# Two-norm prologue of the second block: squares summed on VectorE alone, scaled X in a right-hand pool

## The chip, the cores and the metric

The kernel runs on one core of one Trainium2 chip. The metric is device microseconds of one execution; times of several executions are given by their median. A core has TensorE (PE in the rows, its weight loads PEld), VectorE (DVE), ScalarE (ACT), GpSimd (POOL) and SyncE (SP, which here only issues DMAs). Each engine works through its own queue in order and waits for others by semaphores.

## The reference, cut to what matters

Two model blocks run one after the other on x of 512 positions by 1024 features. The first ends with an expert layer (PEER) and a norm, the second begins with a gated feed-forward layer (FFN) behind a norm of its own:

```python
x = x + gate2 * peer(h2, ...)
x = rmsnorm(x, final_g)                      # end of the first block
x = x + 0.5 * swiglu(rmsnorm_2(x, ffn1_norm), w_gate, w_up, w_down)   # start of the second

def rmsnorm(x, g):
    return x * rsqrt(mean(x * x) + EPS) * g
def swiglu(x, w_gate, w_up, w_down):
    return (silu(x @ w_gate) * (x @ w_up)) @ w_down
```

After it come an attention mixer, a second FFN and a last norm. The two norms at the seam follow directly on each other: the first one's scale is common to a position, so both can be had from two sums over features, of x squared and of (final_g x) squared.

## The kernel before

X lies in SBUF as 8 tiles of 128 features by 512 positions (`X[0]` to `X[7]`). All large products are done in fp32 as three matmuls of rounded halves: `mm3` (lines 102 to 105) multiplies weights `whi`, `wlo` with activations hi, lo. Weights are streamed by SyncE in pieces of 128x1024 into `raw` (3 buffers); `split` (lines 98 to 100) makes `whi` of a piece on ScalarE (L99) and `wlo` on VectorE (L100), each with 3 buffers. `Lin.product` accumulates two PSUM banks `mm` over the 8 feature chunks, that is 48 matmuls from two pieces of weights; there are four `mm` banks.

At the seam, in the order of the program text: VectorE adds the expert layer's result to X (L913); `gains` (lines 203 to 209) makes `gh` on ScalarE (L206) and `gl` on VectorE (L207), the two halves of X times both norms' gains, 16 tiles of 128x512 in the pool `gpool`; `square_two` makes 16 squares on ScalarE (L953), eight with the gain (list `l`) and eight without (list `h`), and adds them up (L955), `l` on VectorE and `h` on GpSimd, 7 adds each. The squares borrow tiles of the FFN's hidden layer, whose pool `ffn` is on the right-hand side of SBUF. `rstd_two` sums each total over partitions by a matmul with ones (L158, first `h`, then `l`), and makes from them `rstd` (both norms together, L963 to L967) and `r3` (the first norm alone, L968 to L970). `scale_x` multiplies X by the first norm (L975, 8 instructions).

In `ffn`, the norm's scale is applied after the products: the gate product of the first 256 hidden columns runs on unscaled `gh`, `gl`; then `rstd` is called; then the up product runs; then `ev_g` (L1025) reads the gate banks from PSUM times `rstd`, and `ev_u` (L1030) the up banks. So with four banks TensorE can do two products before it needs `rstd`; the third waits until L1025 has read the first bank.

This part of the program isn't ordered by hand: a scheduler sets each engine's order from dependences and its own estimates of durations. Pools are stacked from the left or the right end of SBUF, and a tile that lies where an older one lay waits for the older one's last use.

Of the kernel before, what the change touches and what calls it, by code (L numbers as in the profile page):

```python
# [7 lines left out]
F32 = mybir.dt.float32  # L8
# [4 lines left out]
AF = mybir.ActivationFunctionType  # L13
# [5 lines left out]
S = 512  # L19
D = 1024  # L20
P = 128
# [37 lines left out]
def body(nc, tc, A, out, stop=None):  # L59
    from contextlib import ExitStack  # L60
    top = ExitStack()
    pool = lambda stack, name, bufs=1, **kw: stack.enter_context(
        tc.tile_pool(name=name, bufs=bufs, reuse_waits="tile", **kw))
# [11 lines left out]
    tmp = _Tmp()  # L75
# [12 lines left out]
    epst = eps2[:, 0:1]  # L88
# [3 lines left out]
    def col(name, c):  # L92
        o, w = VCOLS[name]
        return vec[:, o + c:o + c + 1]
# [60 lines left out]
    def fsum(ps, chunks):  # L155

        for n, c in enumerate(chunks):
            nc.tensor.matmul(ps, ones, c, start=n == 0, stop=n == len(chunks) - 1)  # L158
        return ps
# [159 lines left out]
    for k in range(DC):  # L319
        if k + 2 < DC:  # L320
            load(k + 2)
        h = tmp.tile([P, S], F32, tag="ht", name="ht", bufs=2)
# [183 lines left out]
    R = lambda stack, name, bufs=1, **kw: pool(stack, name, bufs, side="right", **kw)  # L506
# [11 lines left out]
    for c in range(DC):  # L518
        h = tmp.tile([P, S], F32, tag="ht", name="ht", bufs=2)
# [402 lines left out]
    st2 = ExitStack()  # L922
# [2 lines left out]
    pat = pool(st2, "pat", 1, space=PSUM)  # L925
    lin = Lin(st2, wbufs=3, psum=pmm)
    mp = pool(st2, "mix")
    gpool = pool(st2, "gains")

    def finish():  # L930
        st2.close()
# [8 lines left out]
    def sbank():  # L940

        return pat.tile([P, S], F32, tag="s", name="sum", bufs=2)

    r3 = mp.tile([P, S], F32, name="r3")

    squares = {}

    def square_two(fp):

        for name, eng in (("l", nc.vector), ("h", nc.gpsimd)):  # L950
            for c in range(DC):
                q = fp.tile([P, S], F32, tag=f"hd{name}{FC - 1 - c}", name="sq")
                nc.scalar.activation(q, X[c], AF.Square, scale=col("final_g", c) if name == "l" else 1.0)  # L953
                if c:
                    eng.tensor_add(squares[name], squares[name], q)  # L955
                else:
                    squares[name] = q

    def rstd_two():

        p3 = fsum(sbank(), [squares["h"]])
        sq = tmp.tile([P, S], F32, tag="sd", name="sd", bufs=1)
        nc.vector.tensor_scalar(sq, p3, EPS, EPS * EPS * D, op0=ALU.mult, op1=ALU.add)  # L963
        nc.vector.tensor_add(sq, sq, fsum(sbank(), [squares["l"]]))
        nc.scalar.activation(sq, sq, AF.Sqrt, scale=1.0 / D)
        r = tmp.tile([P, S], F32, tag="rstd", name="rstd", bufs=1)
        nc.vector.reciprocal(r, sq)  # L967
        sd3 = tmp.tile([P, S], F32, tag="ht", name="sd3", bufs=2)  # L968
        nc.scalar.activation(sd3, p3, AF.Sqrt, bias=epst, scale=1.0 / D)
        nc.vector.reciprocal(r3, sd3)  # L970
        return r

    def scale_x():
        for c in range(DC):
            nc.vector.scalar_tensor_tensor(X[c], X[c], col("final_g", c), r3, op0=ALU.mult, op1=ALU.mult)  # L975

# [37 lines left out]
    def ffn(i, hs, rstd, before=None, then=None):  # L1014

        fs = ExitStack()
        fp = R(fs, "ffn")
        hid = [None] * FC
        sl = {}
        if before:  # L1020
            before(fp)

        def ev_g(m, ps):
            sl[m] = fp.tile([P, S], F32, tag="sl", name="sl", bufs=3)
            nc.vector.tensor_mul(sl[m], ps, r)  # L1025
            nc.scalar.activation(sl[m], sl[m], AF.Silu)

        def ev_u(m, ps):
            t = tmp.tile([P, S], F32, tag="ht", name="ht", bufs=2)
            nc.vector.tensor_mul(t, ps, r)  # L1030
            nc.vector.tensor_mul(t, t, sl.pop(m))
            hid[m] = pair(fp, "hd", m)
            split(hid[m][0], hid[m][1], t)
        r = None
        for j in range(FF // 256):
            pg_ = lin.product(A[f"ffn{i}_w_gate_2"], DC, lambda k: hs[k], j)
            r = r or rstd()
            pu_ = lin.product(A[f"ffn{i}_w_up_2"], DC, lambda k: hs[k], j)
            for n in range(2):
                ev_g(2 * j + n, pg_[n])  # L1040
            for n in range(2):
                ev_u(2 * j + n, pu_[n])
            if j == 0 and then:
                then()
            if j == 4 and then:
                mixer_inputs()
        q = Sum2(DC, direct=0 if i == 1 else 2)

        def ev_d(m, ps):
            nc.vector.scalar_tensor_tensor(X[m], ps, 0.5, X[m], op0=ALU.mult, op1=ALU.add)  # L1050
            q.add(X[m])
        lin(A[f"ffn{i}_w_down_2"], FC, lambda k: hid[k], range(4), ev_d)
        fs.close()
        return q

    q = ffn(1, hs, rstd_two, square_two, scale_x)
    if stop == "f1":
        return finish()
# [125 lines left out]
    q = Sum2(DC, direct=0)  # L1184
# [16 lines left out]
    q = ffn(2, hs, lambda: qm.rstd(sbank(), D))  # L1201
# [83 lines left out]
```

## Time and profile before

| | |
|---|---|
| runs | 2621.91, 2624.31, 2623.8 us; median 2623.8 us |
| profiled execution | 2624.25 us, its span 2622.5 us |
| TensorE busy | 2551.2 us, 97% of the span |
| VectorE, ScalarE, GpSimd busy | 1797.8, 1054.8, 425.5 us |
| mean granted TensorE clock | 0.988 of full |
| last of the expert products to the third FFN product | 1579 to 1632 us |

Times in rows are microseconds from the start of the span. "Granted clock" is the share of TensorE's full 2.4 GHz that was granted. In a timeline row the bracket says how long the engine had been idle and whose event ended that; rows of one kind that follow each other are merged with their count.

### The profile page before, as it was taken

The numbers are of one execution on the slowest core, as the hardware profiler recorded it, in microseconds if no ns is written. First come the engines' busy times: TensorE is split into PE (matmuls) and PEld (weight loads), VectorE is DVE, ScalarE is ACT, GpSimd is POOL, SyncE is SP. The second block draws the span as 40 slices with busy tenths as digits, with TensorE's granted clock in tenths as the row PEclk, the third lists the DMA queues.
The fourth block names the chain that finished last, engine by engine and source line by source line (L and its number), as shares of the span: only waits on it lengthen the run. The fifth ranks groups of instructions, "written<-read, shape, count | busy, mean of one in ns | idle before, by whom it ended". The sixth has DMA issues, their size and how long they took to land.

```text
span 2622.5 us, 33272 instructions
## 1 busy us (share of the span) xinstructions
PE 2551.2 (97%) x12311; PEld 2148.2 (82%) x12311; DVE 1797.8 (69%) x3120; ACT 1054.8 (40%) x1759; POOL 425.5 (16%) x323
## 2 busy tenths in 40 slices
PE   8989799999999999999999998999999999999998
PEld 5867589999999988888888886878888675788886
DVE  7999878888987577778888788444334675544423
ACT  4324333467688533333333335222222554422221
POOL 0000231122221233343344321000010000100000
PEclk9999899999999999999999999999999999999999
DMA  7226621678888999999999972222333221222232
GB/s 269 92 94 203 228 73 65 230 237 286 286 293 306 348 362 338 335 330 331 350 340 356 333 284 75 97 89 96 89 97 108 89 73 45 89 96 97 89 96 73
DMA packets 212469, 509.09 MB, mean 194 GB/s; under 512 B 18577, under 2 KB 95889, under 8 KB 212306
## 3 DMA queue, kind: packets, MB, share of 16 engines
q1 hardware_dynamic: 161186, 353.39, 39.7%
q0 software_dynamic: 36864, 134.23, 14.2%
q10 hardware_dynamic: 14256, 19.33, 2.0%
q8 instruction: 97, 1.59, 0.2%
q14 instruction: 66, 0.54, 0.1%
HBM read 461.49 MB, written 45.39 MB: 193 GB/s over the span
## 4 chain that ended last, share of the span: by engine, by line
PE 86%; DVE 7%; ACT 3%; DMA 2%; issue 2%; ACTq 0%; DVEq 0%; SPq 0%
PE mm L103 14%; PE mm L105 14%; PE mm L104 14%; PE pv L105 7%; PE pv L104 7%; PE pv L103 7%; PE act L103 5%; PE act L104 5%; PE act L105 5%; PE mm L338 2%; PE pg L738 2%; PE s L1098 1%; DVE ycv L350 1%; ACT oa L727 1%; PE o L1123 1%
## 5 line engine op out<-in xcount | busy, mean ns | idle before, releaser
L99 ACT CAST whi<-raw 128x1024 fp32r<-128x1024 f32 x228 | 235.5, 1035 | 658.3 <-PE mm L104 537.0
L100 DVE TENSOR_TENSOR wlo<-raw,whi 128x1024 fp32r<-128x1024 f32 x212 | 256.8, 1213 | 326.1 <-ACT whi L99 320.7
L103 PE MATMUL act<-h2h,uhi 128*128 128x384 f32 x1024 | 347.1, 339 | 4.3 <-ACT ga L664 4.1
L104 PE MATMUL mm<-gl,whi 128*128 128x512 f32 x864 | 344.5, 399 | 2.5 <-DVE gl L207 2.4
L105 PE MATMUL mm<-gh,wlo 128*128 128x512 f32 x864 | 342.7, 397 | 1.5 <-DVE wlo L100 1.5
L103 PE MATMUL mm<-gh,whi 128*128 128x512 f32 x864 | 342.5, 397 | 0.4 <-DVE x L913 0.4
L105 PE MATMUL act<-h2h,ulo 128*128 128x384 f32 x1024 | 342.8, 335 | 0.0
L104 PE MATMUL act<-h2l,uhi 128*128 128x384 f32 x1024 | 342.5, 335 | 0.0
L105 PE MATMUL pv<-vhi,cl 128*128 128x512 f32 x768 | 299.6, 390 | 0.0
L104 PE MATMUL pv<-vlo,ch 128*128 128x512 f32 x768 | 299.5, 390 | 0.0
L103 PE MATMUL pv<-vhi,ch 128*128 128x512 f32 x768 | 298.7, 389 | 0.0
L848 DVE TENSOR_TENSOR vlo<-vraw,vhi 128x1024 fp32r<-128x1024 f32 x128 | 156.4, 1222 | 131.6 <-ACT vhi L842 128.8
L694 POOL DMA_INDIRECT row<-in_u_dram,idx x128 | 158.3, 1236 | 526.4 <-DVE act L677 456.8
L694 POOL DMA_INDIRECT row<-in_v_dram,idx x128 | 175.0, 1367 | 284.4 <-DVE gacc L685 262.3
L842 ACT CAST vhi<-vraw 128x1024 fp32r<-128x1024 f32 x128 | 134.4, 1050 | 185.4 <-issue 169.5
L100 DVE TENSOR_TENSOR ulo<-uraw,uhi 128x1024 fp32r<-128x1024 f32 x128 | 156.0, 1220 | 72.7 <-ACT uhi L99 67.7
L103 PEld LDWEIGHTS act<-h2h,uhi 128*128 128x128 f32 x1024 | 192.4, 188 | 7.6 <-ACT ga L664 6.3
L104 PEld LDWEIGHTS mm<-gl,whi 128*128 128x128 f32 x864 | 162.4, 188 | 44.1 <-DVE gl L207 3.8
L103 PEld LDWEIGHTS mm<-gh,whi 128*128 128x128 f32 x864 | 162.3, 188 | 42.6 <-issue 2.3
L105 PEld LDWEIGHTS mm<-gh,wlo 128*128 128x128 f32 x864 | 162.4, 188 | 41.2 <-issue 2.0
L178 POOL TENSOR_TENSOR sq<-sq 128x512 f32<-128x512 f32 x24 | 40.0, 1665 | 952.9 <-ACT sq L172 952.2
L104 PEld LDWEIGHTS act<-h2l,uhi 128*128 128x128 f32 x1024 | 192.4, 188 | 1.3
(835 smaller groups left out, 4884.1 us busy)
## 6 DMA issues: line engine op xcount, KB each, us to landing
uraw<-in_uT_dram SPq DMA_DIRECT2D x128, 512.0 KB
vraw<-in_v_dram SPq DMA_DIRECT2D x128, 512.0 KB
raw<-in_w_in_dram SPq DMA_DIRECT2D x52, 512.0 KB
gsc<-st SPq DMA_DIRECT2D x96, 256.0 KB
vg<-gsc SPq DMA_DIRECT2D x32, 768.0 KB
raw<-in_ffn_w_gate_dram SPq DMA_DIRECT2D x44, 512.0 KB
raw<-in_ffn_w_up_dram SPq DMA_DIRECT2D x44, 512.0 KB
raw<-in_ffn_w_down_dram SPq DMA_DIRECT2D x40, 512.0 KB
```

The source lines that it names most:

```text
L99: nc.scalar.copy(hi, src)
L100: (lo_eng or nc.vector).tensor_sub(lo, src, hi.bitcast(F32))
L103: nc.tensor.matmul(ps, whi, ahi, start=first, stop=False)
L104: nc.tensor.matmul(ps, whi, alo, start=False, stop=False)
L105: nc.tensor.matmul(ps, wlo, ahi, start=False, stop=last)
L178: self.eng.tensor_add(self.acc, self.acc, t)
L338: nc.tensor.matmul(first[m], w[:, m // 2, j:j + P], x, start=k == 0 and w is hi and x is hl[0], stop=k == DC - 1 and w is lo)
L350: nc.vector.scalar_tensor_tensor(ycv[c], glu[c][:, j:j + S], dw(c, j), ycv[c], op0=ALU.mult, op1=ALU.add)
L694: nc.gpsimd.indirect_dma_start(out=r, out_offset=None, in_=A[table], in_offset=bass.IndirectOffsetOnAxis(ap=idx[:, k:k + 1], axis=0))
L738: nc.tensor.matmul(ps[:, :, j], ob[:, 4 * h + j], oa[:, 4 * h + j], start=True, stop=True)
L842: nc.scalar.copy(hi, raw)
L848: nc.vector.tensor_sub(lo, raw, hi.bitcast(F32))
```

## The change

The pool of `gh` and `gl` moves to the right-hand side, where it is now the first that is opened. All 14 adds of squares are on VectorE. The square root and reciprocal that give `r3` move from `rstd_two` into `scale_x`, which is called behind the first FFN evictions.

```diff
-    gpool = pool(st2, "gains")
+    gpool = R(st2, "gains")
...
-        for name, eng in (("l", nc.vector), ("h", nc.gpsimd)):
+        for name in "lh":
...
                 if c:
-                    eng.tensor_add(squares[name], squares[name], q)
+                    nc.vector.tensor_add(squares[name], squares[name], q)
...
         nc.vector.reciprocal(r, sq)
+        squares["p"] = p3
+        return r
+
+    def scale_x():
         sd3 = tmp.tile([P, S], F32, tag="ht", name="sd3", bufs=2)
-        nc.scalar.activation(sd3, p3, AF.Sqrt, bias=epst, scale=1.0 / D)
+        nc.scalar.activation(sd3, squares["p"], AF.Sqrt, bias=epst, scale=1.0 / D)
         nc.vector.reciprocal(r3, sd3)
-        return r
-
-    def scale_x():
         for c in range(DC):
```

The order on VectorE behind the last `gl` (L207), before: `wlo` is a piece of weights, `sd` and `rstd` the way to the joint norm, `r` the first norm's own (`r3`), `x` the tiles of X.

```order
L955 TENSOR_TENSOR sq<-sq 128x512 x5
L100 TENSOR_TENSOR wlo<-raw,whi 128x1024
L1009 TENSOR_TENSOR lam<-lam 128x1
L1010 TENSOR_SCALAR lam<-lam 128x1
L963 TENSOR_SCALAR sd<-sum 128x512
L100 TENSOR_TENSOR wlo<-raw,whi 128x1024
L964 TENSOR_TENSOR sd<-sd,sum 128x512
L970 RECIPROCAL r_14268<-sd_14393 128x512
L967 RECIPROCAL rstd<-sd 128x512
L975 SCALAR_TENSOR_TENSOR x_79<-x_79,vec,r_14268 128x512
L1025 TENSOR_TENSOR sl<-mm,rstd 128x512 x2
```

The same place on VectorE in the change (lines from 972 on are one higher):

```order
L955 TENSOR_TENSOR sq<-sq 128x512 x10
L100 TENSOR_TENSOR wlo<-raw,whi 128x1024
L955 TENSOR_TENSOR sq<-sq 128x512
L100 TENSOR_TENSOR wlo<-raw,whi 128x1024
L955 TENSOR_TENSOR sq<-sq 128x512
L1010 TENSOR_TENSOR lam<-lam 128x1
L1011 TENSOR_SCALAR lam<-lam 128x1
L100 TENSOR_TENSOR wlo<-raw,whi 128x1024
L963 TENSOR_SCALAR sd<-sum 128x512
L964 TENSOR_TENSOR sd<-sd,sum 128x512
L967 RECIPROCAL rstd<-sd 128x512
L100 TENSOR_TENSOR wlo<-raw,whi 128x1024
```

In both, two more adds stand ahead of these rows. The first norm's reciprocal is gone from between L964 and L967; it and the eight scalings of X now stand behind the first evictions (L1026 to L1032). Three pieces' `wlo` now stand ahead of `sd` and a fourth directly ahead of the eviction L1026; before, one stood ahead of `sd` and a second behind it.

On TensorE the two matmuls with ones move. Before, they stand directly behind the 48th matmul of the gate product:

```order
L105 MATMUL mm<-gh_14264,wlo 128x512
L158 MATMUL sum<-sq,ones 128x512 x2
L104 MATMUL mm<-gl_14237,whi 128x512
L105 MATMUL mm<-gh_14236,wlo 128x512
L103 MATMUL mm<-gh_14236,whi 128x512
```

In the change they stand inside the up product:

```order
L103 MATMUL mm<-gh_14252,whi 128x512
L104 MATMUL mm<-gl_14253,whi 128x512
L158 MATMUL sum<-sq,ones 128x512 x2
L105 MATMUL mm<-gh_14252,wlo 128x512
L103 MATMUL mm<-gh_14252,whi 128x512
```

One matmul of the up product stands early in the gate product in both. Behind the gate product, 25 of the up product now come ahead of the sums and 22 behind them; before, all 47 came behind.

## Rows read from the trace of the kernel before

**Rows 1.** The page: busy time and share of the span, TensorE to GpSimd.
```profile
PE 2551.2 (97%) x12311; PEld 2148.2 (82%) x12311; DVE 1797.8 (69%) x3120; ACT 1054.8 (40%) x1759; POOL 425.5 (16%) x323
```

**Rows 2.** The chain that ended last, 1555 to 1640 us: start, length, what.
```profile
1593.05 1.05 ACT sq L953 x2
...
1604.14 3.78 PE sum L158 x4
```

**Rows 3.** Timeline of TensorE: start, length, instruction, idle before and its releaser.
```profile
172.57 0.80 PE L103 MATMUL mm<-hh,whi 128*128 128x512 f32 x1 [4.52 <-ACT whi L99]
...
1586.20 0.50 PE L104 MATMUL mm<-gl,whi 128*128 128x512 f32 x1 [1.24 <-DVE gl L207]
...
1596.80 0.39 PE L105 MATMUL mm<-gh,wlo 128*128 128x512 f32 x1
1604.14 3.78 PE L158 MATMUL sum<-sq,ones 128*128 128x512 f32 x4 [6.95 <-DVE lam L1009]
...
1608.84 0.39 PE L104 MATMUL mm<-gl,whi 128*128 128x512 f32 x1
...
1626.34 0.40 PE L104 MATMUL mm<-gl,whi 128*128 128x512 f32 x1
1628.23 0.74 PE L105 MATMUL mm<-gh,wlo 128*128 128x512 f32 x2 [1.49 <-DVE wlo L100]
...
1643.05 0.40 PE L105 MATMUL mm<-gh,wlo 128*128 128x512 f32 x1
...
2244.14 0.50 PE L104 MATMUL mm<-gl,whi 128*128 128x512 f32 x1 [1.16 <-DVE gl L207]
```

**Rows 4.** Stretches: length, busy us of PE, PEld, DVE, ACT, POOL, clock, DMA.
```profile
172.50:178.00 5.50, 5.39 (x12) 3.81 (x13) 5.45 (x8) 0.02 (x1) 0.00 (x0) 0.50 0.30 95
1604.10:1608.00 3.90, 3.86 (x5) 1.78 (x6) 1.90 (x5) 0.69 (x1) 0.00 (x0) 0.50 0.32 122
1620.00:1632.00 12.00, 10.51 (x45) 8.15 (x44) 10.45 (x14) 2.45 (x4) 0.00 (x0) 1.00 0.21 70
```

**Rows 5.** Timeline of VectorE at the seam.
```profile
1585.40 5.38 DVE L207 SCALAR_TENSOR_TENSOR gl<-x,gg,gh 128x512 fp32r<-128x512 f32 x8
1590.70 0.68 DVE L955 TENSOR_TENSOR sq<-sq 128x512 f32<-128x512 f32 x1
1591.31 0.21 DVE L1005 CUSTOM_DVE_ANT_0 lt<-lt 128x64 f32<-128x64 f32 x1
...
1592.28 8.49 DVE L955 TENSOR_TENSOR sq<-sq 128x512 f32<-128x512 f32 x5
1600.69 2.28 DVE L100 TENSOR_TENSOR wlo<-raw,whi 128x1024 fp32r<-128x1024 f32 x1
...
1606.86 1.22 DVE L100 TENSOR_TENSOR wlo<-raw,whi 128x1024 fp32r<-128x1024 f32 x1
...
1608.59 3.35 DVE L970 RECIPROCAL r<-sd 128x512 f32<-128x512 f32 x1
...
1615.63 1.28 DVE L1025 TENSOR_TENSOR sl<-mm,rstd 128x512 f32<-128x512 f32 x2
```

**Rows 6.** Timeline of GpSimd, 1555 to 1625 us.
```profile
1592.15 11.94 POOL L955 TENSOR_TENSOR sq<-sq 128x512 f32<-128x512 f32 x7 [39.68 <-ACT sq L953]
```

**Rows 7.** Timeline of ScalarE at the seam.
```profile
1590.87 4.26 ACT L953 ACTIVATE sq<-x 128x512 f32<-128x512 f32 x8
1595.04 1.04 ACT L99 CAST whi<-raw 128x1024 fp32r<-128x1024 f32 x1
1596.10 1.28 ACT L1007 ACT_TABLE_LOAD   x1
...
1613.52 1.05 ACT L99 CAST whi<-raw 128x1024 fp32r<-128x1024 f32 x1 [4.18 <-PE mm L104]
```

**Rows 8.** Timeline of TensorE at a later sum with ones, at full clock.
```profile
2251.02 1.02 PE L158 MATMUL sum<-sq,ones 128*128 128x512 f32 x2
...
2252.11 0.41 PE L104 MATMUL mm<-gl,whi 128*128 128x512 f32 x1
```

More of the change, by code (lines that the diff above doesn't have):

```diff
@@ L967, in rstd_two @@
         nc.vector.reciprocal(r, sq)
-        sd3 = tmp.tile([P, S], F32, tag="ht", name="sd3", bufs=2)
-        nc.scalar.activation(sd3, p3, AF.Sqrt, bias=epst, scale=1.0 / D)
-        nc.vector.reciprocal(r3, sd3)
+        squares["p"] = p3
         return r
     def scale_x():
+        sd3 = tmp.tile([P, S], F32, tag="ht", name="sd3", bufs=2)
+        nc.scalar.activation(sd3, squares["p"], AF.Sqrt, bias=epst, scale=1.0 / D)
+        nc.vector.reciprocal(r3, sd3)
         for c in range(DC):
```

## The prediction

> **What bounds the kernel now.** I read the page's busy shares first: TensorE is busy 97% of the span, the next engine 69% [rows 1]. So a change can gain only where TensorE stands still or runs at half clock. The chain that ended last, read around the seam between the blocks, is TensorE's except for one stretch: it leaves TensorE for ScalarE's squares and VectorE's queue and comes back at 1604.14 with the sums over partitions [rows 2]. TensorE's timeline shows the hole: the last matmul of the gate product starts at 1596.80, the next instruction, a sum with ones, at 1604.14 [rows 3]. The stretches then give the clock: 0.50 of full, that is 1.2 GHz, from 1604.10 to 1608.00 [rows 4].
>
> Who is late? VectorE's five adds in a row take 8.49 us, 1.70 each, while GpSimd does its seven in 11.94, from 1592.15 to 1604.09 [rows 5, 6]. The add just before, with GpSimd silent, took 0.68 and let the next instruction start 0.61 after it; `wlo` took 2.28 beside GpSimd and 1.22 alone [rows 5]. The two engines slow each other, and the first sum, which needs GpSimd's total, starts 0.05 us after GpSimd ends.
>
> **The account of the stretch before.** Fix two points: the slot behind the gate product, 1597.03 (1596.80 and one matmul slot), and the slot behind the second up product, 1643.28, one slot after the row at 1643.05 [rows 3]. A slot is 0.233 us: 75 of them from 1608.84 to 1626.34 [rows 3]. Between the points lie 143 matmuls (47 of the first up product, 48 and 48), 33.4 us of the 46.25. The other 12.9 are: 7.1 waiting for the sums; 4.0 from 1604.14 to 1608.84 beyond the three slots in it, which is the two sums at half clock and the restart; 1.8 in the hole that ends at 1628.23, for a `wlo` behind the scalings of X [rows 3].
>
> **The change, part by part.**
> - *Adds.* GpSimd's 7 adds go; VectorE gets 14 at 0.61 (the row at 1590.70), as nothing disturbs it. Its path from 1590.70: 14 adds 8.5, the two small `lam` pairs 0.4 (0.2 each by the row at 1591.31), two `wlo` at 1.2: the last add ends at 1602.0 [rows 5]. ScalarE is not late for it: its squares end at 1595.1, and two casts behind them take 1.05 each [rows 7]. The bounds are 0.61 and 1.70 an add; I take the near one, from the same instruction with GpSimd idle.
> - *Sums moved.* 25 matmuls of the up product now fill TensorE from 1597.03 to 1602.86. The totals are ready at 1602.0, so the wait of 7.1 goes. TensorE never stops, so the sums run at full clock: the later pair of records of one sum and one matmul took 1.09 from 2251.02 to 2252.11 [rows 8], so a sum is 0.86 and two 1.72. They end at 1604.58, and the 22 matmuls left of the up product at 1609.7.
> - *The way to `rstd`.* VectorE: `wlo` of the third piece, whose cast waits until TensorE has left the buffer near 1602.6, ends at about 1604.9; two instructions of the adds' size 1.2; the square root on ScalarE 0.7 (a square takes 4.26 / 8 = 0.53 [rows 7], and it starts on an empty queue); one reciprocal 3.3 instead of two [rows 5]. `rstd` is there at about 1610.1.
> - *The new wait.* Between `rstd` and the eviction L1026 now stands a fourth `wlo`. Its piece's `whi` may be cast only when TensorE has done the last matmul that reads that buffer, at the end of the up product: 1609.65. Cast 1.05 [rows 7] to 1610.8, `wlo` 1.2 to 1612.0. The eviction starts then, and TensorE about 0.8 after it, as after the first `gl` (1585.40, then 1586.20) [rows 3, 5]: 1612.8. That third product needs the bank, so TensorE waits 3.1 us, a wait that was not there before, when the eviction began at 1615.63 [rows 5], ahead of the up product's end.
> - *First norm's own scale.* Square root, reciprocal (3.35) and eight scalings of X now stand behind the first evictions. VectorE is through with them at about 1628; the bank they hold up is needed at the end of the second up product, 1635, and the next `wlo` stands ahead of the scalings, done at 1623 against a need at 1629.6. So the hole of 1.8 goes too. If VectorE were 6 us later there, it would come back.
> - *Table loads.* ScalarE gets two more at 1.28 [rows 7], around the moved square root; the casts behind them have at least 5 us.
> - *The pool.* The new place lets `gh`, `gl` lie where earlier right-hand pools lay and the squares further in. The added waits are for instructions of the expert layer, done before 1580; in the trace `gh` waits for X alone. Worth nothing either way; the gains' store order on ScalarE shifts by one square, 0.6, ahead of nothing that is late.
>
> Sum: 12.9 before; after it 1.7 for the sums and 3.1 of new wait; gain 8.1 us. Behind 1643 the orders of both kernels are the same, and TensorE's longest hole there is the 1.16 us at 2244.14 [rows 3], so the gain stays. The profiled execution took 2624.25 us, 1.75 beyond its span; it lies 0.45 above the median of the runs. Against the median 2623.8 the sum gives **2615.7 us**, 0.3% less. A measurement of this kernel tells about 0.2%, 5.2 us, from no change.
>
> **The clock, which speaks against the sum.** A stop of 1.49 us left the clock at 1.00; one of 4.52 us was followed by 0.50 for 5.5 us [rows 3, 4]. The new wait of 3.1 lies between them, nearer the first. If the clock falls there, the price is that of the restart at 1604.14: 4.70 us to 1608.84 for work worth 1.72 and three slots, so 2.3. The Trainium skill, "TensorE: Matmul & The Clock Gate", section on the HAM clock gate, takes half rate as the default that only activity lifts; by that rule an idle TensorE pays again at each restart, the gain would be 5.8, and the row at 172.57 agrees with it, the one at 1628.23 does not.
>
> **Rivals.**
> 1. *The clock falls in the new wait*: 8.1 less 2.3, 2618.0 us. For it: the length lies between the two rows. Against: it is nearer the shorter one, and TensorE is full before it.
> 2. *Half the gain*: adds that depend on each other take nearer 0.7 to 0.8, or the small `lam` instruction is as slow as its neighbours; the sums are up to 2 us late and `rstd` takes the place of `wlo` as the last event; or the hole behind the scalings stays. About 4 us gained, 2619.8.
> 3. *Nothing*: the pool's new place makes `gh` or a square wait for a late reader, or the time is lost again later; 2623.8. Against it: no such wait has a late source by the trace.
> 4. *Slower*: VectorE becomes the bound. If adds cost 1.70 and `wlo` 2.28 on VectorE for another reason than GpSimd, its last add ends at 1590.7 + 1.2 + 0.4 + 12 x 1.70 + 4.6 = 1617.3. TensorE stands from 1602.9 to then, restarts at half clock (sums 3.4), ends the up product at about 1626.4, waits 3.1, and reaches the second point 22.4 later, at 1651.9: 8.6 behind, 2632.4 us. It decides from about 1.1 us an add: sums at 1608.7 and a lost clock eat the 8.1. Against it stand the rows at 1590.70 and 1606.86.
>
> **How the numbers follow.** Chances: the forecast 0.60, rival 1 0.17, rival 2 0.09, rival 3 0.10, rival 4 0.04. The range reaches from 2613.5 (a new wait 1 us shorter, and a run 1 us low; the runs spread over 2.4) to 2620.5, which takes in rivals 1 and 2 and leaves out 0.14 and the tails. Faster by over 0.2% means below 2618.6: the forecast and about two thirds of rival 1, 0.70. Within 0.2%: the rest of rival 1, rivals 2 and 3, 0.26. Slower: rival 4, 0.04.
>
> **What would show it.** Right: L955 fourteen times on VectorE at 0.6 to 0.7; no idle TensorE before L158, the two sums in about 1.7 at clock 1.00; one idle of about 3 us before the third product, released by VectorE's L1026; none at the middle of the second up product; the slot behind that product near 1635. Wrong: idle before L158, adds over 1 us, a new idle over 4 us with 0.50 behind it, or holes behind 1635 that make up for the gain.

## The result and the profile after

The change takes the kernel from 2624.06 to 2602.36 us (medians of four runs each). The ratio, which leaves out one disturbed run of the new kernel, is 0.9913, 95% interval 0.9900 to 0.9927. The gain is 22 us; the forecast was 8, and its range ended at 2613.5. The profiled execution took 2602.71 us with a span of 2600.9, 21.6 less than before.

**Where did it go?** First the seam. TensorE's timeline of the kernel after, with the columns of [rows 3]:

```profile
1585.79 0.50 PE L104 MATMUL mm<-gl,whi 128*128 128x512 f32 x1 [1.24 <-DVE gl L207]
...
1596.11 0.39 PE L105 MATMUL mm<-gh,wlo 128*128 128x512 f32 x1
1596.34 0.39 PE L104 MATMUL mm<-gl,whi 128*128 128x512 f32 x1
...
1602.38 1.96 PE L158 MATMUL sum<-sq,ones 128*128 128x512 f32 x4 [0.21 <-DVE lam L1010]
...
1612.27 0.47 PE L103 MATMUL mm<-gh,whi 128*128 128x512 f32 x1 [2.90 <-DVE sl L1026]
...
1615.51 0.63 PE L105 MATMUL mm<-gh,wlo 128*128 128x512 f32 x1
1615.94 0.44 PE L103 MATMUL mm<-gh,whi 128*128 128x512 f32 x1
1616.21 0.40 PE L104 MATMUL mm<-gl,whi 128*128 128x512 f32 x1
...
1635.52 0.39 PE L105 MATMUL mm<-gh,wlo 128*128 128x512 f32 x1
...
2229.53 0.50 PE L104 MATMUL mm<-gl,whi 128*128 128x512 f32 x1 [1.15 <-DVE gl L207]
```

The wait of 6.95 us before the sums [rows 3] is down to 0.21, the hole of 1.49 in the second up product is gone, and a new wait of 2.90 stands before the third product. VectorE and ScalarE, with the columns of [rows 5, 7], show why:

```profile
1591.87 6.88 DVE L955 TENSOR_TENSOR sq<-sq 128x512 f32<-128x512 f32 x10
...
1601.55 0.69 DVE L955 TENSOR_TENSOR sq<-sq 128x512 f32<-128x512 f32 x1
...
1605.92 3.35 DVE L967 RECIPROCAL rstd<-sd 128x512 f32<-128x512 f32 x1 [0.70 <-ACT sd L965]
1610.29 1.23 DVE L100 TENSOR_TENSOR wlo<-raw,whi 128x1024 fp32r<-128x1024 f32 x1 [1.02 <-ACT whi L99]
1611.44 1.28 DVE L1026 TENSOR_TENSOR sl<-mm,rstd 128x512 f32<-128x512 f32 x2
```

```profile
1609.22 1.04 ACT L99 CAST whi<-raw 128x1024 fp32r<-128x1024 f32 x1 [3.33 <-PE mm L104]
```

Ten adds take 6.88 us, 0.69 each, where five took 8.49 beside GpSimd [rows 5], which now does none of them. Then comes the new wait as the prediction drew it: the cast waits for TensorE, the fourth `wlo` for the cast, the eviction L1026 stands behind it.

The stretches, with the columns of [rows 4], give the clock: full in the sums, about half behind the new wait, full again.

```profile
1602.00:1604.40 2.40, 2.19 (x6) 1.06 (x6) 2.25 (x5) 1.86 (x2) 0.00 (x0) 1.00 0.79 263
1612.27:1616.00 3.73, 3.73 (x10) 2.95 (x11) 3.64 (x7) 2.55 (x5) 0.00 (x0) 0.54 0.41 141
1620.00:1635.00 15.00, 15.00 (x68) 12.43 (x67) 11.08 (x14) 5.08 (x6) 0.00 (x0) 1.00 0.30 95
```

Between the prediction's two fixed points lie 39.41 us now (1596.34 to 1635.75, one slot behind the row at 1635.52), where there were 46.25. So the seam gave 6.8 us of 21.6. Where is the rest? The marker at 2244.14 [rows 3] is 14.6 earlier, the end 21.6. Another 7 us were gained between the second fixed point and that row, and 7 more from there to the end, with no hole in either beyond the one at the marker itself (1.16 and 1.15 us). TensorE was full before and is full now, so it must be doing the same work faster. Two stretches of 100 us in the second feed-forward say so, of before and of after:

```profile
2300.00:2400.00 100.00, 100.00 (x430) 80.48 (x429) 44.14 (x54) 28.98 (x36) 0.00 (x0) 1.00 0.28 95
```

```profile
2300.00:2400.00 100.00, 100.00 (x443) 82.81 (x442) 43.79 (x53) 29.11 (x36) 0.00 (x0) 1.00 0.30 100
```

Busy 100.00 and clock 1.00 in both, but 443 matmuls for 430. VectorE's evictions mark the period: L1030 before, L1031 after, once per gate and up product (96 matmuls); L1050 and L1051 once per down product (132). Before, then after:

```profile
1665.18 1.39 DVE L1030 TENSOR_TENSOR ht<-mm,rstd 128x512 f32<-128x512 f32 x2 [2.79 <-PE mm L105]
...
1687.58 1.39 DVE L1030 TENSOR_TENSOR ht<-mm,rstd 128x512 f32<-128x512 f32 x2 [2.79 <-PE mm L105]
...
1875.73 1.37 DVE L1050 SCALAR_TENSOR_TENSOR x<-mm,x 128x512 f32<-128x512 f32 x2
...
1905.65 1.37 DVE L1050 SCALAR_TENSOR_TENSOR x<-mm,x 128x512 f32<-128x512 f32 x2
```

```profile
1657.03 1.37 DVE L1031 TENSOR_TENSOR ht<-mm,rstd 128x512 f32<-128x512 f32 x2 [2.63 <-PE mm L105]
...
1678.79 1.37 DVE L1031 TENSOR_TENSOR ht<-mm,rstd 128x512 f32<-128x512 f32 x2 [2.63 <-PE mm L105]
...
1862.43 1.37 DVE L1051 SCALAR_TENSOR_TENSOR x<-mm,x 128x512 f32<-128x512 f32 x2
...
1892.35 1.37 DVE L1051 SCALAR_TENSOR_TENSOR x<-mm,x 128x512 f32<-128x512 f32 x2
```

A gate and up pair took 22.40 us and takes 21.76: a slot of 0.2333 became 0.2267. The down product takes 29.92 in both, 0.2267 a slot. Only matmuls that stream `gh` and `gl` got faster, and those are the tiles that the pool moved. At 0.0067 each, the 1056 of the second feed-forward alone are worth 7.0 us. Between the second fixed point and the marker, by the starts in the two traces, the matmuls that stream `gh` and `gl` take 7.8 us less. The 384 of the attention's value product, in which `gh` and `gl` are the weights and `whi`, `wlo` are streamed in 256 columns, take 0.8 more.

What is different about the new place? In the compiled programs, `gh0` starts at byte 91456 of its partition before and at 196576 after; `hd` and the weight pieces `whi`, `wlo` start elsewhere, but all at remainder 224 when divided by 256. Every one of these tiles is a multiple of 256 bytes long, so all of a kind share a remainder: for `gh` and `gl` it was 64, and is now 224, that of the weights. Below, two tiles are called in step when these remainders agree.

### The profile page after: what moved, and what is told of

The parts are those of the page before. It is cut to its first block, busy times and chain, and to the rows that moved or that the text cites. A ratio compares the mean times of both kernels' runs of the same rounds, so it can differ in the third digit from the quotient of the medians.

```text
span 2600.9 us, 33262 instructions
## 1 busy us (share of the span) xinstructions
PE 2535.3 (97%) x12311; PEld 2149.1 (83%) x12311; DVE 1794.5 (69%) x3127; ACT 1058.2 (41%) x1761; POOL 413.7 (16%) x316
## 4 chain that ended last, share of the span: by engine, by line
PE 85%; DVE 7%; ACT 3%; DMA 2%; issue 2%; ACTq 0%; SPq 0%; DVEq 0%
PE mm L103 14%; PE mm L105 14%; PE mm L104 14%; PE pv L104 7%; PE pv L105 7%; PE pv L103 7%; PE act L103 5%; PE act L105 5%; PE act L104 5%; PE mm L338 2%; PE pg L738 2%; PE s L1099 1%; DVE ycv L350 1%; ACT oa L727 1%; PE o L1124 1%
## 5 line engine op out<-in xcount | busy, mean ns | idle before, releaser
L103 PE MATMUL act<-h2h,uhi 128*128 128x384 f32 x1024 | 347.1, 339 | 4.3 <-ACT ga L664 4.1
L105 PE MATMUL act<-h2h,ulo 128*128 128x384 f32 x1024 | 342.8, 335 | 0.0
L103 PE MATMUL mm<-gh,whi 128*128 128x512 f32 x864 | 339.5, 393 | 3.3 <-DVE sl L1026 2.9
L104 PE MATMUL act<-h2l,uhi 128*128 128x384 f32 x1024 | 342.5, 335 | 0.0
L104 PE MATMUL mm<-gl,whi 128*128 128x512 f32 x864 | 338.4, 392 | 2.8 <-DVE gl L207 2.8
L105 PE MATMUL mm<-gh,wlo 128*128 128x512 f32 x864 | 338.8, 392 | 0.0
L103 PE MATMUL pv<-vhi,ch 128*128 128x512 f32 x768 | 298.8, 389 | 1.1 <-ACT ch L847 1.1
L105 PE MATMUL pv<-vhi,cl 128*128 128x512 f32 x768 | 299.6, 390 | 0.0
L104 PE MATMUL pv<-vlo,ch 128*128 128x512 f32 x768 | 299.5, 390 | 0.0
L103 PEld LDWEIGHTS act<-h2h,uhi 128*128 128x128 f32 x1024 | 192.4, 188 | 7.6 <-ACT ga L664 6.3
L103 PEld LDWEIGHTS mm<-gh,whi 128*128 128x128 f32 x864 | 162.6, 188 | 40.3 <-issue 5.8
L104 PEld LDWEIGHTS mm<-gl,whi 128*128 128x128 f32 x864 | 162.6, 188 | 38.2 <-DVE gl L207 4.1
L104 PEld LDWEIGHTS act<-h2l,uhi 128*128 128x128 f32 x1024 | 192.4, 188 | 1.3
L105 PEld LDWEIGHTS act<-h2h,ulo 128*128 128x128 f32 x1024 | 192.2, 188 | 0.0
```

The source lines that it names most:

```text
L103: nc.tensor.matmul(ps, whi, ahi, start=first, stop=False)
L104: nc.tensor.matmul(ps, whi, alo, start=False, stop=False)
L105: nc.tensor.matmul(ps, wlo, ahi, start=False, stop=last)
```

## The experiments

**Side or start address? Pool or adds?** The first four runs split the change in two, and shift the gains by 32 bytes on either side. Theory A at that time took the remainder by 64 for what counts (32 fast, 0 slow).

The kernel before, gains on the left, shifted:

```diff
     gg = mp.tile([P, DC], F32, name="gg")
+    pad = mp.tile([P, 8], F32, name="pad")
```

> The kernel before with 32 bytes of unused pad in front of the gains, so that gh and gl stay on the left but start at 32 past a multiple of 64 bytes, as they do after the change; adds and order stay as before. Theory A (the matmul slot hangs on the start address of the moving tile): slot of a gate/up matmul 0.2267 us where it was 0.2333, the seam as before, about 2609 us. Theory B (it hangs on the side or region of SBUF in which gh and gl lie): slot 0.2333, about 2624 us.

Ratio to before 0.9999 (0.9990 to 1.0009). The kernel after, gains on the right, shifted:

```diff
+    R(st2, "edge").tile([P, 8], F32, name="edge")
     gpool = R(st2, "gains")
+    pad = gpool.tile([P, 8], F32, name="pad")
```

> The kernel after, with 32 bytes in front of the gains on the right, so that gh and gl lie on the right at multiples of 64 bytes; the tiles hd stay at 32 past one. Theory A: gate/up slot 0.2333 us again, about 2616 to 2617 us (near the forecast of the prediction). Theory B: slot 0.2267, about 2602 us.

Ratio 0.9994 (0.9985 to 1.0004): 2623 us, outside both theories. VectorE's evictions, of the first run and of the second:

```profile
1662.58 1.40 DVE L1031 TENSOR_TENSOR ht<-mm,rstd 128x512 f32<-128x512 f32 x2 [2.75 <-PE mm L105]
...
1684.89 1.38 DVE L1031 TENSOR_TENSOR ht<-mm,rstd 128x512 f32<-128x512 f32 x2 [2.76 <-PE mm L105]
```

```profile
1652.88 1.39 DVE L1033 TENSOR_TENSOR ht<-mm,rstd 128x512 f32<-128x512 f32 x2 [2.78 <-PE mm L105]
...
1675.28 1.39 DVE L1033 TENSOR_TENSOR ht<-mm,rstd 128x512 f32<-128x512 f32 x2 [2.78 <-PE mm L105]
...
1864.24 1.39 DVE L1053 SCALAR_TENSOR_TENSOR x<-mm,x 128x512 f32<-128x512 f32 x2
...
1895.04 1.39 DVE L1053 SCALAR_TENSOR_TENSOR x<-mm,x 128x512 f32<-128x512 f32 x2
```

The first gives 22.31 us per 96, a mean slot of 0.2324: hardly better, and in its second feed-forward it is 22.40 again, 0.2333. The second has 22.40 again, though it lies on the right, and its down product fell to 30.80 per 132, 0.2333. There the 64 bytes that I put ahead of `hd` had moved `hd` too, from remainder 224 to 160 by 256. So both theories fell: the side does not help, and 32 by 64 does not do. Only 224 had been fast.

The pool alone, and the adds alone:

```diff
-    gpool = pool(st2, "gains")
+    gpool = R(st2, "gains")
```

> The kernel before with the gains' pool on the right and nothing else: half the adds on GpSimd, r3 ahead of the evictions. If the pool gives what the seam does not explain: gate/up slot 0.2267 us, the wait of about 7 us before the sums still there, about 2609 us. If the gain comes with the adds and the order: slot 0.2333, about 2624 us.

Ratio 0.9944 (0.9927 to 0.9960), some 15 us, with the old seam still there:

```profile
1604.50 3.78 PE L158 MATMUL sum<-sq,ones 128*128 128x512 f32 x4 [6.20 <-POOL sq L955]
...
1628.78 0.74 PE L105 MATMUL mm<-gh,wlo 128*128 128x512 f32 x2 [3.30 <-DVE wlo L100]
```

> The kernel after with the gains' pool on the left as before: all adds on VectorE, r3 behind the evictions. The prediction's own sum, without the pool: 2615.7 to 2618 us, the latter with the clock falling in the new wait; gate/up slot 0.2333 us. If the adds carried the whole gain: about 2602 us.

(The kernel after, with that line put back.) 2614.85 us, ratio 0.9953 (0.9936 to 0.9970), 11 to 12 us: even more than the sum, and for a reason that its timeline shows. The wait before the third product is not there:

```profile
1603.09 1.88 PE L158 MATMUL sum<-sq,ones 128*128 128x512 f32 x4
...
1612.36 0.48 PE L103 MATMUL mm<-gh,whi 128*128 128x512 f32 x1 [0.40 <-DVE sl L1026]
```

With the pool on the left the scheduler puts the third piece's cast behind the square root L965 and the fourth behind that; the fourth `wlo` then stands behind L1026 and L1031, and the eviction does not wait for it:

```profile
1611.54 1.27 DVE L1026 TENSOR_TENSOR sl<-mm,rstd 128x512 f32<-128x512 f32 x2
1612.73 1.28 DVE L1031 TENSOR_TENSOR ht<-mm,rstd 128x512 f32<-128x512 f32 x2
1613.93 1.22 DVE L100 TENSOR_TENSOR wlo<-raw,whi 128x1024 fp32r<-128x1024 f32 x1
```

The wait that the prediction priced belongs to the order of casts that comes with the pool on the right.

**Which address, then?** Two theories were left: the moving tile must start at 224 (A), or weights and moving tile must share their remainder (R). Here `Lin` gets an unused tile ahead of its weight pieces (a new argument, used in the second block alone); the first of the two runs also moves the tiles on the right.

```diff
+            if pad:
+                pool(stack, "wpad").tile([P, 8], F32, name="wpad")
...
+    R(st2, "edge").tile([P, 56], F32, name="edge")
     gpool = R(st2, "gains")
```

> The kernel after with the weight pieces of the second block moved up by 32 bytes, from remainder 224 to 0 by 256, and gh, gl and hd moved down by 224 bytes, from 224 to 0: weights and moving tiles share one remainder again, but another one. Runs so far: remainder 224 beside weights at 224 gave a slot of 0.2267 us; 64, 192, 160 beside 224 gave 0.2333; 96 beside 224 gave 0.2324 on average. Theory R (the two remainders by 256 must agree): slot 0.2267, about 2602 us. Theory A (the moving tile must start at 224): slot 0.2333 in gate, up and down, about 24 us more than the kernel after (2592 and 1056 matmuls at 0.0067), 2626 us.

> The kernel after with the weight pieces of the second block alone moved up by 32 bytes, to remainder 0; gh, gl and hd stay at 224. Theory R (remainders must agree): slot 0.2333 in gate, up and down, about 24 us more than the kernel after, 2626 us. Theory A (the moving tile must start at 224): slot 0.2267, 2602 us.

All at 0: 2603.52 us, ratio 0.9912 (0.9895 to 0.9928), the same as after. Weights alone at 0: 2626.14, ratio 0.9999 (0.9989 to 1.0008); nothing is left of the whole change, since its seam gain is paid again by the down products. The stretch 2300 to 2400 us, of the first and of the second:

```profile
2300.00:2400.00 100.00, 100.00 (x443) 82.81 (x442) 43.68 (x52) 29.05 (x36) 0.00 (x0) 1.00 0.29 99
```

```profile
2300.00:2400.00 100.00, 100.00 (x430) 80.49 (x429) 45.44 (x56) 29.11 (x36) 0.00 (x0) 1.00 0.28 95
```

R holds in both, A in neither.

**The gains on the left, in step.** If R holds, 160 bytes of pad do on the left what the pool on the right does.

```diff
     gg = mp.tile([P, DC], F32, name="gg")
+    pad = mp.tile([P, 40], F32, name="pad")
```

> The kernel before with 160 bytes of unused pad ahead of the gains: they stay on the left, at remainder 224 by 256, the weights' own. Theories A and R both: slot 0.2267, some 14 to 15 us less than before, like the run with the pool alone on the right. Theory B (it is the right-hand side of SBUF that helps): slot 0.2333, no gain.

> The kernel after with the gains on the left as before, 160 bytes of pad ahead of them (remainder 224), and so with the order of casts that the run of the adds alone had: there the eviction stood ahead of the fourth wlo, and TensorE waited 0.40 us and kept its clock where after waits 2.90 and loses 2.9 more to half clock. If both hold together: slot 0.2267, a wait under 1 us before the third product, about 5 us below the kernel after, 2597 us. If the short wait was due to the slower matmuls alone (they end the up product later): wait of about 1 to 3 us, 2599 to 2602 us.

In the kernel before: 2610.47 us, ratio 0.9939 (0.9922 to 0.9955), the pool's whole gain with the pool where it was. In the kernel after with its pool put back: 2597.46 us, ratio 0.9893 (0.9877 to 0.9910), the best of the study, about 6 us below the run at remainder 0 in the same comparison, which has the slots and the seam of the kernel after. The 6 are rough: with four runs each, the two intervals overlap. Its seam, on TensorE, and its clock behind the short wait:

```profile
1599.42 1.96 PE L158 MATMUL sum<-sq,ones 128*128 128x512 f32 x4
...
1608.78 0.47 PE L103 MATMUL mm<-gh,whi 128*128 128x512 f32 x1 [0.59 <-DVE sl L1027]
```

```profile
1608.78:1612.00 3.22, 3.22 (x14) 2.69 (x15) 3.22 (x5) 2.75 (x4) 0.00 (x0) 1.00 0.48 163
```

A wait of 0.59 where after had 2.90, and the clock stays at full in this trace. So the short wait was due to the order of casts, not to slower matmuls. Against the trace of the kernel after, the span is 5.0 us shorter: 2.3 of it is this wait and 1.7 the half clock, where the expectation had put 2.9.

**Which reads clash?** Three more runs, timed once each, have one kind of tile out of step by 32 bytes.

```diff
             hi = self.s.tile([P, 4, 256], F32R, tag="whi", name="whi")
+            if self.pad:
+                self.s.tile([P, 8], F32, tag="pad2", name="pad2", bufs=1)
+                self.pad = False
```

> The kernel after with wlo alone moved up by 32 bytes (remainder 0); whi, gh, gl and hd stay at 224. Which weights does a streaming matmul clash with? Slots are taken from start to start, in the second block's products. Theory own: the matmul's own weights; the matmul of L105 (wlo) is long, 0.247 us or 0.233, L103 and L104 short, 0.2267. Theory next: the weights that are loaded meanwhile for the following matmul; L104, which is followed by wlo, is long, L103 and L105 short. Either way about a third of the 24 us: some 2610 us.

> The mirror image: whi alone at remainder 0, wlo back at 224 like gh, gl and hd. Theory own: L103 and L104 long (both take whi), L105 short. Theory next: L103 and L105 long (each is followed by whi), L104 short. About two thirds of the 24 us: some 2618 us.

(The second has the pad of 8 ahead of `whi` and one of 56 behind it.) They took 2626.16 and 2625.15 us: neither a third nor two thirds, but the whole. With `wlo` alone out of step the mean start-to-start times in the down products were 0.233, 0.239 and 0.228 us behind L103, L104 and L105 (352 each, from the trace's starts in nanoseconds), 0.700 for the three, as with all weights out of step. With `whi` alone they were nearly even, 0.232, 0.231 and 0.233, 0.696 for the three. *Own* falls: it has L105 long in the first run and short in the second, and it is the other way round. *Next* has the order right (L104 the longest in the first, the shortest in the second), but all six lie above 0.2267, so it does not say why the whole price is paid.

```diff
+        if name == "g":
+            return (pl.tile([P, S], F32R, tag=f"gh{c}", name=f"gh{c}", bufs=bufs),
+                    pl.tile([P, S + 64], F32R, tag=f"gl{c}", name=f"gl{c}", bufs=bufs)[:, 8:8 + S])
```

> The kernel after with the tiles gl alone read 32 bytes further on (remainder 0); gh, hd, whi and wlo stay at 224. One of the three matmuls of each group then reads a moving tile out of step. If a product pays in full for one tile out of step, as in the two runs with whi or wlo alone: slot 0.232 to 0.233 us on average in gate, up and the query and key products (2592 matmuls), down stays at 0.2267, about 17 us more than after, 2617 to 2620 us. If it pays by the matmul: a third of that, about 2608 us.

2620.81 us. Gate and up, then down:

```profile
1660.88 1.39 DVE L1034 TENSOR_TENSOR ht<-mm,rstd 128x512 f32<-128x512 f32 x2 [2.78 <-PE mm L105]
...
1683.28 1.39 DVE L1034 TENSOR_TENSOR ht<-mm,rstd 128x512 f32<-128x512 f32 x2 [2.78 <-PE mm L105]
...
1871.39 1.37 DVE L1054 SCALAR_TENSOR_TENSOR x<-mm,x 128x512 f32<-128x512 f32 x2
...
1901.31 1.37 DVE L1054 SCALAR_TENSOR_TENSOR x<-mm,x 128x512 f32<-128x512 f32 x2
```

22.40 per 96: one matmul of three out of step, and the product pays in full (0.236 behind L104, which streams `gl`, 0.232 behind the other two), while the down product, whose tiles agree, keeps 29.92.

| run | weights | `gh`, `gl` | `hd` | slot gate/up, us | slot down, us |
|---|---|---|---|---|---|
| before, adds alone | 224 | 64 | 224 | 0.2333 | 0.2267 |
| after, pool alone, both runs with 160 bytes on the left | 224 | 224 | 224 | 0.2267 | 0.2267 |
| left, 32 bytes | 224 | 96 | 224 | 0.2324, then 0.2333 | 0.2267 |
| right, 32 bytes | 224 | 192 | 160 | 0.2333 | 0.2333 |
| both 0 | 0 | 0 | 0 | 0.2267 | 0.2267 |
| weights 0 | 0 | 224 | 224 | 0.2333 | 0.2333 |
| `wlo` 0 | 224, 0 | 224 | 224 | 0.2333 | 0.2333 |
| `whi` 0 | 0, 224 | 224 | 224 | 0.2318 | 0.2319 |
| `gl` 0 | 224 | 224, 0 | 224 | 0.2333 | 0.2267 |

(Remainders of the start byte by 256; two values are those of the high and the low half, or of the first and the second feed-forward.) A difference of 128 bytes, in the run with 32 on the left, is out of step; one of 256 costs nothing: in the kernel after, the weights start at remainder 224 by 512 and `gh`, `gl` at 480. Why TensorE is slower out of step stays open: whether two reads meet and which, and why the three matmuls pay together.

## Why the prediction was wrong

**The step that failed** is the last of its parts, "The pool ... Worth nothing either way." It looked for waits that the move adds and found none, rightly; it did not ask at which address the tiles would start. The pool alone gives 14 to 15 us. The premise behind it, in the first paragraph, failed too: that a change can gain only where TensorE stands still or runs at half clock. Busy throughout and at clock 1.00 both times, TensorE did 443 matmuls in 100 us in place of 430. Nothing on the page of before names it: TensorE was "busy", and the account of the stretch took 0.233 us as *the* slot, though the down products of the same trace ran at 0.2267. Two slots for the same shape in one profile were the sign to read.

The other steps, by their own numbers:

- *Adds*: forecast at 0.61 from start to start, with the last ending at 1602.0. Ten took 0.68 each and the other four 0.6, in all 0.7 us more than forecast; the last still ended at 1602.2, as the first began 0.4 earlier. Right in the mechanism.
- *Sums moved*: forecast behind 25 up matmuls with no stop, at full clock. TensorE stood still for 0.21 us before them, and they ran at clock 1.00. Right.
- *The way to `rstd` and the new wait*: forecast 1610.1 and 3.1 us with TensorE back at 1612.8; the reciprocal started at 1605.92 and ended near 1609.3, 0.8 earlier; the wait was 2.90 and TensorE was back at 1612.27, by the chain that was forecast.
- *First norm's own scale, table loads*: the hole in the second up product is gone and nothing is late for them. Right.
- *The clock*: the forecast took it as kept, rival 1 as lost, and rival 1 was right. The ten matmuls from 1612.27 to 1616.21 took 3.94 us where ten slots are 2.27: 1.7 us, against its 2.3. The Trainium skill's page cited there ("TensorE: Matmul & The Clock Gate", Part 1, on the HAM clock gate) has half rate as the default, and the clock of 0.54 from 1612.27 agrees. That each restart pays, as the prediction took from it, does not hold: behind the wait of 0.59 the clock stayed at 1.00.

Net of slots the seam had 12.9 us and has 39.41 less 143 slots of 0.2267, 7.0. So the waits gave 5.9, rival 1's 5.8 almost to the tenth, though with two errors that cancel: the sums and the stop before them took 2.4 for 1.7, the new wait and its clock 4.6 for 5.4. That the adds alone came to 2614.85, near the forecast of 2615.7, is luck: beside their own before of 2625.81 they gained 11 us, not 8.1, as the wait that the sum prices is not there. The range failed on the pool, a term that it did not hold at all. Of the total of 21.6 us in the span, 5.9 are waits at the seam, 15.0 slots (0.9 within the seam, 7.1 and 7.0 behind it, the 0.8 of the value product taken off), and 0.7 had come before the first point.

The two halves also meet. Pool alone times adds alone would be 0.9944 x 0.9953 = 0.9897, about what the shifted left pool gives (0.9893). The kernel after has 0.9913: its pool on the right brings the order of casts with the 2.90 us wait and the half clock behind it.

## What to carry to other kernels

Where TensorE is full, compare the slots of equal matmuls in different products before costing anything else; a slot that differs by 3% on 2592 matmuls was worth more here than every wait at the seam. When a change moves a tile that a matmul reads, work out its start byte beside that of the other operand, and try a pad that puts it in step: 160 bytes were worth 15 us here. Measure it, as the value product lost by it. And a pool that moves can change the scheduler's order on other engines, so price the order as it comes out.

## What the runs showed of the hardware

For 128x512 matmuls with fp32r operands back to back at full clock, the slot was 0.2267 us when stationary and moving tiles started at the same remainder by 256 bytes (shown for remainders 224 and 0, on either side of SBUF for 224), and 0.2318 to 0.2333 when any one kind of tile differed, by 32, 64, 128 or 160 bytes. For the 384 matmuls of 256 columns in the value product it was the other way round: the median start-to-start time was 0.120 us in the five kernels in step and 0.117 to 0.119 in the eight others. So the rule is shown for the 512-column matmuls alone.

The Trainium skill's page "SBUF — State Buffer", section Specifications (TRN2), speaks of 16-byte cachelines and a penalty at each crossing; every start here is a multiple of 32, so by that rule all places would be alike, and the runs differ.

TensorE's clock fell behind the new wait of about 2.9 us in each of the seven kernels that had it (0.54 in the kernel after), and stayed at 1.00 behind waits of 0.40 and 0.59. But the length of a wait does not decide alone. In five kernels (32 bytes on the left, adds alone, both at 0, `whi` 0, `gl` 0) the clock also fell to half at the start of the first gate product, where TensorE has two short waits, 0.42 and 1.24 us; in the eight others, the kernels before and after among them, it stayed at 1.00 there. In three (adds alone, `wlo` 0, `gl` 0) it stayed at 1.00 behind 2.23 us ahead of the second feed-forward. Below are the run with `whi` at 0 and the run with `wlo` at 0, each with the restart (columns of [rows 3]) and the stretch behind it (columns of [rows 4]):

```profile
1588.96 0.79 PE L104 MATMUL mm<-gl,whi 128*128 128x512 f32 x1 [1.25 <-DVE gl L213]
...
1588.96:1591.00 2.04, 2.04 (x5) 1.65 (x6) 2.04 (x4) 2.04 (x5) 0.00 (x0) 0.50 0.00 0
```

```profile
2242.67 0.50 PE L104 MATMUL mm<-gl,whi 128*128 128x512 f32 x1 [2.23 <-DVE gl L211]
...
2242.67:2246.67 4.00, 4.00 (x17) 3.28 (x18) 2.49 (x3) 1.05 (x1) 0.00 (x0) 1.00 0.21 83
```

So what decides, for waits up to 2.9 us, stays open.
